# One stream of gate units beside three seven-product pairs, and state updates in pairs of rows, in a two-layer trunk on one Trainium2 core

## The chip, the cores and the metric

The kernel runs on one core of a Trainium2 chip. The metric is the device time of one execution in microseconds (us); lower is better. Engines are named as in the profile: PE is TensorE (PEld its weight loads), DVE is VectorE, ACT is ScalarE, POOL is GpSimd, and SP is SyncE, which here only issues DMAs.

## The reference

Two layers work on x of 256 tokens by 2048, in float32. Layer 0 (even) has a gated linear recurrence and a dilated attention and is not touched. Layer 1 (odd) is this:

```python
def odd_layer(x, norm, w_in, w_alpha, b_alpha, head_norm, v_norm, w_s, b_s, w_out):
    h = rms_norm(x, norm)
    z = h @ w_in
    q, k, v, a_lr, gc, u, vd, gd = jnp.split(z, split_points(ODD_SIZES), axis=-1)
    log_a = jax.nn.log_sigmoid((a_lr @ w_alpha + b_alpha).astype(F32)) / GLA_TAU
    o = gla_chunked(heads(q, GLA_DK), heads(k, GLA_DK), heads(v, GLA_DV), heads(log_a, GLA_DK))
    yc = rms_norm(o, head_norm).reshape(bsz, seq, GLA_VW).astype(x.dtype) * jax.nn.silu(gc)
    yd = spatial_gating(jax.nn.gelu(u), jax.nn.gelu(vd), w_s, b_s, v_norm) * jax.nn.silu(gd)
    return jnp.concatenate([yc.astype(x.dtype), yd.astype(x.dtype)], axis=-1) @ w_out
```

`gla_chunked` has four heads and four chunks of 64 tokens. Its state goes from chunk to chunk as decay * state + upd, with upd = (k * exp(b_last - b))^T v of one chunk; the output of a chunk is its masked product with v plus q times the state before it. The kernel ends with x + layer 1, normalized.

## The kernel before

Each product with a float32 weight is made of three matmuls on halves: activations and weights are split into a rounded high part and the rest, and high*high, high*low and low*high are added in PSUM. A weight tile comes as one DMA of 128 x 1024 (512 KB) into a slot of `rawp` (10 slots). `parts` (L122) makes its halves: ACT casts it to `whi` (L125, 4 slots) and DVE subtracts to `wlo` (L73, 4 slots). The raw slot is free when the subtraction has ended.

A *unit* is 512 columns of `w_in`. `token_steps` (L146) computes one: 8 steps, each with one weight tile, its two halves of 512 columns and, for both token blocks, three matmuls each (L133 to L135), 12 matmuls of 512 columns. `by_token` runs such steps alone.

`pair` (L199) computes two units together by seven products instead of eight (a Strassen scheme over two token blocks, two units and two halves of the rows). Its 28 steps each have one weight tile and 6 matmuls (L227 to L229): steps 1 to 4 on tiles x0, 5 to 8 on y0, 9 to 12 on x0, 13 to 16 on y0, 17 to 20 on x0, 21 to 24 on z0, 25 to 28 on x0. The sums of weights are made by the DMAs: after the halves of a tile are made, POOL issues a DMA that adds another weight tile to it in place (L221, 16 per pair), and the tile is used again 8 steps later. x0 and y0 are loaded ahead (L214), z0 behind step 16, so a pair holds eight raw slots of the ten. The sums of activations are made once for all three pairs by `make_forms` (L679) on DVE and ACT, in 8 pieces; the first pair needs the first of them at its fifth step.

Side work is written as generators. `spawn` starts one; a yield of n gives way until n ticks have passed; `tick` is called with the matmuls, two ticks per pair step and four per token step of 512 columns. `drain` runs all that is left. The order in which an engine gets its instructions is then made by the framework's scheduler, which puts them roughly in program order and moves one ahead when it reckons that its inputs are ready.

Layer 1 runs in this order: `w_va` (a quarter of v and the decay's input, 272 columns), unit 0 (another quarter of v, 256 columns), with `make_forms` and `decay` (L630) as side work; then `weave` (L169) of the pair of q and k with units 2 (half of v) and 22 (half of the gate gc), 16 token steps spread over the 28 pair steps; `gla` (L759) as side work of the second pair (vd), which has no unit beside it; then the third pair (u) with units 26 (rest of gc) and 38 (half of gd), 16 token steps; then unit 42 (rest of gd) alone; then `w_out1`. At the third pair's start `gla_gate(0)` and `normed` begin as side work; `gla_gate(1)` begins when unit 26 is done. Constants `vn` and `hn` (512 KB each in SBUF) are loaded by POOL between the second and the third pair, `wst` between the first and the second.

PSUM has eight banks in three pools: `psm` (4, the products of by_token and pair), `psa` (2, transposes and small products), `pso` (2, products of units beside a pair, state updates `up` of L787, outputs `op`, and `s_ps`).

Of the kernel before, what the change touches and what calls it, by code (L numbers as in the profile page):

```python
# [16 lines left out]
P = 128  # L17
# [34 lines left out]
def trunk(ctx, tc, x, xt, lead, w_in0, w_out0, w_va, w_in1, w_out1, w_gate, small, dist, cst, w_alpha, w_s,  # L52
# [28 lines left out]
    def big_tile(shape, name):  # L81
        return big.tile(shape, F32, name=name, tag="big")
# [83 lines left out]
            yield  # L166
        return ps

    def weave(pair_steps, units):  # L169

        total, done, taken = 28, 0, 0
        units = list(units)
        count = 8 * len(units)
        result = None
        while True:
            try:
                next(pair_steps)
            except StopIteration as end:
                result = end.value
                break  # L180
            taken += 1
            while units and done * total < taken * count:
                steps, use = units[0]
                try:
                    next(steps)
                    done += 1
                except StopIteration as end:
                    use(end.value)
                    units.pop(0)
        for steps, use in units:  # L190
            while True:
                try:
                    next(steps)
                except StopIteration as end:
                    use(end.value)
                    break
        return result

    def pair(w, ua, ub, act, forms):  # L199

# [476 lines left out]
    forms2 = [(sums2, k0, b) for k0, b in ((0, 0), (8, 0), (8, 1), (0, 1))]  # L677

    def make_forms():  # L679
        for i in range(2):  # L680
            def part(k0, b, lo=0):
                return act2[:, k0 + 4 * i:k0 + 4 * i + 4, lo + b * P:lo + (b + 1) * P].bitcast(F32)

            def plus(o, a, b, op=ALU.add):
                nc.vector.tensor_tensor(out=o, in0=a, in1=b, op=op)  # L685

            def minus(o, a, b):
                plus(o, a, b, ALU.subtract)

            def keep(f, src):  # L690
                _, k0, b = forms2[f]
                split(sums2, slice(k0 + 4 * i, k0 + 4 * i + 4), b * P, P, src)

            s, r = (sp_tile([P, 4, P], n) for n in ("fs", "fr"))
            minus(s, part(0, 1), part(8, 1))
            minus(r, part(0, 1, T), part(8, 1, T))
            plus(s, s, r)
            keep(1, s)
            yield 3
            minus(r, part(0, 0), s)  # L700
            plus(r, r, part(0, 0, T))
            keep(2, r)
            yield 3
            minus(s, part(8, 0), r)
            plus(s, s, part(8, 0, T))
            keep(0, s)
            yield 3
            s, r = (sp_tile([P, 4, P], n) for n in ("fs", "fr"))
            minus(s, part(0, 1), part(0, 0))
            minus(r, part(0, 1, T), part(0, 0, T))  # L710
            plus(s, s, r)
            keep(3, s)
            yield 3
# [9 lines left out]
    ps = by_token(w_in1, 0, act2, n=256)  # L723
    for b in range(2):
        nc.scalar.activation(v1[0][:, b, 256:512], ps[b], AF.Copy, scale=rs1[:, b:b + 1])
    gates = [None, None]

    def spare():
        return [pso.tile([P, 512], F32, name="ps2", tag="o") for _ in range(2)]

    def unit_between(unit, use):
        return token_steps(w_in1, unit, act2, ps=spare()), use

    def keep_v1(ps):
        for b in range(2):
            nc.scalar.activation(v1[1][:, b, :], ps[b], AF.Copy, scale=rs1[:, b:b + 1])

    def keep_gate(c):
        def use(ps):
# [2 lines left out]
                nc.scalar.activation(gates[c][:, b, :], ps[b], AF.Silu, scale=rs1[:, b:b + 1])  # L742
        return use

    ps, ps_k = weave(pair(w_in1, 6, 10, act2, forms2), [unit_between(2, keep_v1), unit_between(22, keep_gate(0))])
    drain()
    eb, enb, ebl = decays
    for b in range(2):
# [2 lines left out]
    for b in range(2):  # L751
        for t in (enb, ebl):
            nc.vector.scalar_tensor_tensor(out=t[:, b, :], in0=ps_k[b], scalar=rs1[:, b:b + 1], in1=t[:, b, :],
                                           op0=ALU.mult, op1=ALU.mult)
    qt, kt, kd = eb, enb, ebl
    osb = []
    gla_ro = []

    def gla():  # L759
# [21 lines left out]
        st = [big_tile([P, 4, T], f"st{c}") for c in range(3)]  # L781
        for h in range(4):
            vs = slice((h % 2) * T, (h % 2) * T + T)
            for c in range(3):
                lo = (c % 2) * 64
                up = pso.tile([P, T], F32, name="up", tag="o")
                nc.tensor.matmul(up, kd[lo:lo + 64, c // 2, h * P:(h + 1) * P], v1[h // 2][lo:lo + 64, c // 2, vs],  # L787
                                 start=True, stop=True)
                if c == 0:
                    nc.scalar.copy(st[0][:, h, :], up)  # L790
                else:
                    nc.vector.scalar_tensor_tensor(out=st[c][:, h, :], in0=st[c - 1][:, h, :],
                                                   scalar=dec[:, h, c:c + 1], in1=up, op0=ALU.mult, op1=ALU.add)
                yield 1
        osb.extend(big_tile([P, 2, 512], f"osb{b}") for b in range(2))
        sso = tiny.tile([P, 2, 4], F32, name="sso", tag="sso", bufs=1)
        for b in range(2):
            for hp in range(2):
                op = pso.tile([P, 2, T], F32, name="op", tag="o")
                for i in range(2):  # L800
                    h = 2 * hp + i
                    vs = slice(i * T, (i + 1) * T)
                    if b:
                        nc.tensor.matmul(op[:, i, :], att[:, b, h, :], v1[hp][:, b, vs], start=True, stop=False)
                    for half in range(2):
                        c = 2 * b + half
                        own = slice(half * 64, half * 64 + 64)
                        if not b:
                            nc.tensor.matmul(op[own, i, :], att[:, b, h, own], v1[hp][:, b, vs],
                                             start=True, stop=(c == 0))  # L810
                        if c:
                            nc.tensor.matmul(op[own, i, :], qtt[:, h, b * P + half * 64:b * P + half * 64 + 64],
                                             st[c - 1][:, h, :], start=False, stop=True)
                nc.scalar.copy(osb[b][:, hp, :], op)
                for i in range(2):
                    square_sum(osb[b][:, hp, i * T:(i + 1) * T], sso[:, b, 2 * hp + i:2 * hp + i + 1])
                yield 2
# [8 lines left out]
                            base=0, channel_multiplier=-1)  # L826
    vf = []
    mv = tiny.tile([P, 8, 2], F32, name="mv", tag="mv", bufs=1)
    for c, ps in enumerate(weave(pair(w_in1, 14, 18, act2, forms2), [])):
        t = big_tile([P, 2, 512], f"vf{c}")  # L830
        for b in range(2):
            nc.scalar.activation(t[:, b, :], ps[b], AF.Gelu_apprx_tanh, scale=rs1[:, b:b + 1])
            for i in range(2):
                bs = tiny.tile([P, 6], F32, name="bs", tag="bs", bufs=2)
                nc.vector.bn_stats(bs, t[:, b, i * T:(i + 1) * T])
                nc.vector.bn_aggr(mv[:, c * 4 + b * 2 + i, :], bs)
        vf.append(t)
# [41 lines left out]
    yd = []  # L879
    spawn(gla_gate(0))  # L880
    spawn(normed(0))
    spawn(normed(1))

    def mix(c, t):
        yield 2
        for b in range(2):
            s_ps = pso.tile([P, 2, T], F32, name="s_ps", tag="o")
            for i in range(2):
                g = 2 * c + i
                nc.tensor.matmul(s_ps[:, i, :], wst[:, g, :], vf[c][:, b, i * T:(i + 1) * T], start=True, stop=True)  # L890
                nc.vector.scalar_tensor_tensor(out=t[:, b, i * T:(i + 1) * T], in0=s_ps[:, i, :],
                                               scalar=sm[:, S_BS + g:S_BS + g + 1], in1=t[:, b, i * T:(i + 1) * T],
                                               op0=ALU.add, op1=ALU.mult)
            yield 2

    def keep_gate1(ps):
        keep_gate(1)(ps)
        spawn(gla_gate(1))

    sgds = [big_tile([P, 2, 512], "sgd0")]  # L900

    def keep_gd0(ps):
        for b in range(2):
            nc.scalar.activation(sgds[0][:, b, :], ps[b], AF.Silu, scale=rs1[:, b:b + 1])

    between = [unit_between(26, keep_gate1), unit_between(38, keep_gd0)]
    for c, ps in enumerate(weave(pair(w_in1, 30, 34, act2, forms2), between)):
        t = big_tile([P, 2, 512], f"yd{c}")
        for b in range(2):
            nc.scalar.activation(t[:, b, :], ps[b], AF.Gelu_apprx_tanh, scale=rs1[:, b:b + 1])  # L910
        yd.append(t)
        spawn(mix(c, t))
# [11 lines left out]


    spawn(sgu_gate(0, 16))
    ps = by_token(w_in1, 42, act2)
    sgds.append(big_tile([P, 2, 512], "sgd1"))
    for b in range(2):
        nc.scalar.activation(sgds[1][:, b, :], ps[b], AF.Silu, scale=rs1[:, b:b + 1])  # L930
    spawn(sgu_gate(1, 1))


# [148 lines left out]
```

## Time and profile before

| | us |
|---|---|
| median of 3 runs | 894.34 (893.6 to 894.72) |
| the profiled execution | 894.46 |
| its span, first to last instruction | 892.7 |
| PE busy | 866.1 (97%) |
| DVE busy | 596.0 (67%) |
| ACT busy | 528.4 (59%) |
| POOL busy | 55.3 (6%) |

The busy time is that of one profiled execution. PE's matmuls are pipelined and their ends are modelled, so a busy PE is not PE at its peak. A wait is put down to whatever ended it. Layer 1 begins near 485 us; its pairs run from about 522, 609 and 671 us on, and the last weights' product ends near 885 us.

### The profile page before, as it was taken

The page shows a single profiled execution, that of the slowest core. Times are in us where ns is not written, and L with a number is a line of the kernel's source. Part 1 is how long each engine was busy: PE and PEld are TensorE (multiplying, and loading weights), DVE is VectorE, ACT ScalarE, POOL GpSimd, SP SyncE. Part 2 cuts the span into 40 slices and gives each one's busy share as a digit, 9 for nine tenths or more (in the row PEclk, how much of TensorE's full clock was granted, in tenths as well). Part 3 has the DMA queues.
Part 4 walks back from the last instruction along what each step waited for, and adds up shares of the span by engine and source line. Part 5 has one row for each costly group of instructions (what it writes and reads, how often), then busy time and mean ns, then how long its engine had stood idle before and what let it go on. Part 6 is the DMA issues. An engine that isn't in the chain of part 4 may idle for free.

```text
span 892.7 us, 11928 instructions
## 1 busy us (share of the span) xinstructions
PE 866.1 (97%) x4408; PEld 725.8 (81%) x4408; DVE 596.0 (67%) x851; ACT 528.4 (59%) x765; POOL 55.3 (6%) x75
## 2 busy tenths in 40 slices
PE   9999999999999999999999799999995999999996
PEld 7888888888888888888888688887574877888886
DVE  7676556586586587666555976687477668665652
ACT  7755556766766756554444586656573556754542
POOL 0100000000000000000000012103111211000000
PEclk9999999999999999999999899999997999999999
DMA  9886655455465365565545479999996999665502
GB/s 345 340 330 207 196 185 165 154 183 174 139 201 166 118 208 175 192 195 188 189 123 168 140 178 251 298 299 216 233 248 175 227 307 307 224 221 193 193 26 94
DMA packets 52138, 182.35 MB, mean 204 GB/s; under 512 B 5856, under 2 KB 6368, under 8 KB 51824
## 3 DMA queue, kind: packets, MB, share of 16 engines
q1 hardware_dynamic: 43776, 152.13, 49.4%
q0 software_dynamic: 8160, 29.40, 16.7%
q8 instruction: 34, 0.56, 0.2%
q14 instruction: 24, 0.20, 0.1%
q10 hardware_dynamic: 144, 0.07, 0.0%
HBM read 179.47 MB, written 2.10 MB: 203 GB/s over the span
## 4 chain that ended last, share of the span: by engine, by line
PE 85%; DMA 6%; DVE 5%; ACT 2%; issue 1%; ACTq 0%; DVEq 0%
PE pc L272 20%; PE ps L134 13%; PE ps L135 12%; PE ps L133 12%; PE pc L271 10%; DMA raw<-in_w_in 6%; PE ps L227 3%; PE ps L229 3%; PE ps L228 3%; DVE wlo L73 2%; ACT whi L125 1%; PE up L787 1%; PE pc L274 1%; DVE fs L685 1%; PE sc L457 1%
## 5 line engine op out<-in xcount | busy, mean ns | idle before, releaser
L73 DVE TENSOR_TENSOR wlo<-raw,whi 128x1024 fp32r<-128x1024 f32 (+1 forms) x320 | 384.0, 1211 | 206.1 <-ACT whi L125 194.5
L125 ACT CAST whi<-raw 128x1024 fp32r<-128x1024 f32 (+1 forms) x320 | 330.3, 1041 | 262.2 <-PE ps L135 102.7
L272 PE MATMUL pc<-act,whi 128*128 128x512 f32 x768 | 269.7, 395 | 0.0
L271 PE MATMUL pc<-act,wlo 128*128 128x256 f32 x720 | 208.7, 290 | 0.0
L272 PEld LDWEIGHTS pc<-act,whi 128*128 128x128 f32 x768 | 142.8, 188 | 29.2
L134 PE MATMUL ps<-wlo,act 128*128 128x512 f32 (+2 forms) x352 | 134.3, 382 | 9.0 <-DVE wlo L73 9.0
L133 PE MATMUL ps<-whi,act 128*128 128x512 f32 (+2 forms) x352 | 133.0, 382 | 7.2 <-ACT whi L125 6.8
L271 PEld LDWEIGHTS pc<-act,wlo 128*128 128x128 f32 x720 | 136.0, 189 | 2.5 <-DVE wlo L73 0.9
L135 PE MATMUL ps<-whi,act 128*128 128x512 f32 (+2 forms) x352 | 133.2, 379 | 0.0
L133 PE MATMUL ps<-whi,yt 128*128 128x512 f32 (+1 forms) x256 | 97.1, 379 | 0.0
L135 PE MATMUL ps<-whi,yt 128*128 128x512 f32 (+1 forms) x256 | 96.4, 377 | 0.0
L134 PE MATMUL ps<-wlo,yt 128*128 128x512 f32 (+1 forms) x256 | 96.3, 376 | 0.0
L134 PEld LDWEIGHTS ps<-wlo,act 128*128 128x128 f32 x352 | 68.4, 194 | 22.1 <-DVE wlo L73 10.7
L133 PEld LDWEIGHTS ps<-whi,act 128*128 128x128 f32 x352 | 67.5, 193 | 20.5 <-ACT whi L125 7.8
L135 PEld LDWEIGHTS ps<-whi,act 128*128 128x128 f32 x352 | 68.4, 194 | 11.4
L221 POOL DMA_DIRECT2D raw<-in_w_in x48 | 41.2, 858 | 308.4 <-DMA raw<-in_w_in 148.1
L135 PEld LDWEIGHTS ps<-whi,yt 128*128 128x128 f32 x256 | 48.2, 188 | 8.9
L134 PEld LDWEIGHTS ps<-wlo,yt 128*128 128x128 f32 x256 | 48.2, 188 | 8.5
L133 PEld LDWEIGHTS ps<-whi,yt 128*128 128x128 f32 x256 | 48.2, 188 | 8.4
L227 PE MATMUL ps<-whi,sums 128*128 128x512 f32 x96 | 39.4, 410 | 0.0
L228 PE MATMUL ps<-wlo,sums 128*128 128x512 f32 x96 | 37.6, 392 | 0.0
L229 PE MATMUL ps<-whi,sums 128*128 128x512 f32 x96 | 37.6, 391 | 0.0
(271 smaller groups left out, 894.1 us busy)
## 6 DMA issues: line engine op xcount, KB each, us to landing
raw<-in_w_in SPq DMA_DIRECT2D x204, 512.0 KB, 5.0
raw<-in_w_out SPq DMA_DIRECT2D x64, 512.0 KB, 4.6
raw<-in_w_in POOLq DMA_DIRECT2D x48, 512.0 KB, 8.7
raw<-in_w_va SPq DMA_DIRECT2D x8, 272.0 KB, 2.6
xs<-in_x SPq DMA_DIRECT2D x2, 1024.0 KB, 5.8
out<-xs SPq DMA_DIRECT2D x8, 256.0 KB, 2.6
first<-in_lead SPq DMA_DIRECT2D x4, 384.0 KB, 4.9
xt<-in_xt SPq DMA_DIRECT2D x6, 256.0 KB, 7.8
```

The lines of the kernel that those rows point to most:

```text
L73: nc.vector.tensor_tensor(out=o, in0=a, in1=hi.bitcast(F32), op=ALU.subtract)
L125: nc.scalar.copy(hi, raw)
L133: nc.tensor.matmul(ps[b], xh, wh, start=first, stop=False)
L134: nc.tensor.matmul(ps[b], xh, wl, start=False, stop=False)
L135: nc.tensor.matmul(ps[b], xl, wh, start=False, stop=last)
L221: nc.gpsimd.dma_start(out=raw, in_=part(u, i), accum_op=ALU.add)
L227: nc.tensor.matmul(ps, xh, wh, start=(first and j == 0), stop=False, skip_group_check=not first)
L228: nc.tensor.matmul(ps, xh, wl, start=False, stop=False, skip_group_check=not first)
L229: nc.tensor.matmul(ps, xl, wh, start=False, stop=(j == 7), skip_group_check=not first)
L271: nc.tensor.matmul(ps[c][:, 1, :], wl, act[:, k, 0:T], start=False, stop=False)
L272: nc.tensor.matmul(ps[c], wh, act[:, k, :], start=(k == 0), stop=(k == KT - 1))
L274: nc.tensor.matmul(ps[c][:, 1, :], wl, act[:, k, 0:T], start=False, stop=False)
```

## The change

Unit 2 (half of v) moves ahead of the first pair and runs alone, so v is whole before the pairs. A class `Stream` holds one row of four units (22, 26, 38, 42: both halves of gc, both of gd) and gives out their steps one by one; `weave` takes 12 of them beside the first pair, 4 beside the second and 12 beside the third, and `stream.finish()` runs the last 4 behind it. `make_forms` begins 6 ticks later. `gla_gate(1)` starts with `gla_gate(0)`. The state updates of chunks 0 and 1 are issued next to each other, on the two halves of the rows; that of chunk 2 takes all 128 rows, for which the second half of `kd`'s second block (chunk 3) is set to zero by POOL. `up`, `op` and `s_ps` move from `pso` to `psa`; `pso` is left to the units.

```diff
+    class Stream:
+        def step(self):
+            if not self.units:
+                return
+            steps, use = self.units[0]
+            if callable(steps):
+                steps = steps()
+                self.units[0] = steps, use
+                self.left = 8
+            next(steps)
+            self.left -= 1
+            if not self.left:
+                self.units.pop(0)
...
+    def weave(steps, stream, count):
+        done = taken = 0
+        while True:
+            try:
+                next(steps)
+            except StopIteration as end:
+                return end.value
+            taken += 1
+            while done * 28 < taken * count:
+                stream.step()
+                done += 1
...
     def make_forms():
+        yield 6
...
+    ps = by_token(w_in1, 2, act2)
+    for b in range(2):
+        nc.scalar.activation(v1[1][:, b, :], ps[b], AF.Copy, scale=rs1[:, b:b + 1])
...
+    stream = Stream([between(22, keep_gate(0)), between(26, keep_gate(1)), between(38, keep_gd(0)),
+                     between(42, keep_gd(1))])
+    ps, ps_k = weave(pair(w_in1, 6, 10, act2, forms2), stream, 12)
     drain()
...
+    nc.gpsimd.memset(kd[64:P, 1, :], 0.0)
...
-            for c in range(3):
-                lo = (c % 2) * 64
-                up = pso.tile([P, T], F32, name="up", tag="o")
...
+            ups = [psa.tile([P, T], F32, name="up", tag="a") for _ in range(2)]
+            for c in range(2):
+                own = slice(c * 64, c * 64 + 64)
+                nc.tensor.matmul(ups[c], kd[own, 0, h * P:(h + 1) * P], v1[h // 2][own, 0, vs], start=True, stop=True)
+            nc.scalar.copy(st[0][:, h, :], ups[0])
+            nc.vector.scalar_tensor_tensor(out=st[1][:, h, :], in0=st[0][:, h, :], scalar=dec[:, h, 1:2], in1=ups[1],
+                                           op0=ALU.mult, op1=ALU.add)
+            yield 2
+            up = psa.tile([P, T], F32, name="up", tag="a")
+            nc.tensor.matmul(up, kd[:, 1, h * P:(h + 1) * P], v1[h // 2][:, 1, vs], start=True, stop=True)
+            nc.vector.scalar_tensor_tensor(out=st[2][:, h, :], in0=st[1][:, h, :], scalar=dec[:, h, 2:3], in1=up,
+                                           op0=ALU.mult, op1=ALU.add)
+            yield 2
...
-                op = pso.tile([P, 2, T], F32, name="op", tag="o")
+                op = psa.tile([P, 2, T], F32, name="op", tag="a")
...
-    for c, ps in enumerate(weave(pair(w_in1, 14, 18, act2, forms2), [])):
+    for c, ps in enumerate(weave(pair(w_in1, 14, 18, act2, forms2), stream, 4)):
...
     spawn(normed(0))
+    spawn(gla_gate(1))
     spawn(normed(1))
...
-            s_ps = pso.tile([P, 2, T], F32, name="s_ps", tag="o")
+            s_ps = psa.tile([P, 2, T], F32, name="s_ps", tag="a")
...
-    for c, ps in enumerate(weave(pair(w_in1, 30, 34, act2, forms2), between)):
+    for c, ps in enumerate(weave(pair(w_in1, 30, 34, act2, forms2), stream, 12)):
...
     spawn(sgu_gate(0, 16))
-    ps = by_token(w_in1, 42, act2)
+    stream.finish()
     spawn(sgu_gate(1, 1))
```

## Rows read from the trace of the kernel before

**Rows 1.** Busy time by stage: stretch, length, engines (x instructions), granted clock, DMA, GB/s.

```profile
484.00:522.00 38.00, 32.10 (x214) 29.22 (x213) 34.95 (x55) 24.12 (x36) 0.90 (x1) 0.91 0.47 147
609.00:671.00 62.00, 61.10 (x271) 40.57 (x268) 41.67 (x51) 40.13 (x60) 13.96 (x17) 1.00 0.99 234
671.00:692.00 21.00, 12.13 (x38) 9.17 (x39) 16.72 (x38) 7.58 (x8) 1.94 (x3) 0.76 0.60 158
```

**Rows 2.** PE's waits, 484 to 522: who, for whom, total us, times, longest.

```profile
PE ps L134 <- DVE wlo L73: 4.8, 3, 3.1
PE ps L133 <- ACT whi L125: 1.0, 1, 1.0
```

**Rows 3.** PE's waits from 609 to 745.

```profile
PE ps L133 <- ACT whi L125: 5.8, 2, 5.5
PE ps L134 <- DVE wlo L73: 4.0, 2, 3.2
PE ps L228 <- DVE wlo L73: 0.8, 2, 0.5
```

**Rows 4.** Busy time and granted clock of three stretches at half clock.

```profile
498.40:504.20 5.80, 5.72 (x25) 5.72 (x26) 5.60 (x10) 1.89 (x4) 0.00 (x0) 0.51 0.59 191
676.40:681.60 5.20, 5.17 (x14) 3.97 (x15) 3.04 (x4) 4.05 (x4) 0.87 (x1) 0.50 0.45 115
688.50:691.80 3.30, 3.27 (x8) 2.59 (x9) 3.30 (x4) 0.00 (x0) 0.88 (x2) 0.50 0.52 161
```

**Rows 5.** Chain of waits, 664 to 706: start, us, engine or DMA, tile.

```profile
665.62 9.61 DMA raw<-in_w_in
...
692.51 8.35 DMA raw<-in_w_in
...
703.30 8.57 DMA raw<-in_w_in
```

**Rows 6.** Timeline of PE, first pair: start, us; a token step, then two pair steps.

```profile
541.73 0.40 PE L133 MATMUL ps<-whi,act 128*128 128x512 f32 x1
...
544.47 0.39 PE L227 MATMUL ps<-whi,sums 128*128 128x512 f32 x1
...
547.19 0.39 PE L133 MATMUL ps<-whi,act 128*128 128x512 f32 x1
```

**Rows 7.** Timeline of PE: two state updates in a row, of 12.

```profile
617.57 0.70 PE L787 MATMUL up<-vv,ebl 64*128 64x256 f32 x2
...
619.09 0.70 PE L787 MATMUL up<-vv,ebl 64*128 64x256 f32 x2
```

**Rows 8.** Chain of waits: a float32 matmul of 128 rows in layer 0.

```profile
151.27 0.43 PE gp L540 x2
```

**Rows 9.** Timeline of PE, 636 to 637: matmuls of 64 columns.

```profile
636.51 0.38 PE L809 MATMUL op<-vv,att 128*64 128x256 f32 x1
636.52 0.38 PE L812 MATMUL op<-st,qtt 128*64 128x256 f32 x1
```

**Rows 10.** Tile `up`, who reads it: ns min/median/max, first and last start.

```profile
L792 DVE SCALAR_TENSOR_TENSOR st<-st,dec,up x8: 475/478/481, 619.9 to 635.1; 128x256 f32<-128x256 f32 x8
```

**Rows 11.** Groups of instructions, 484 to 522: count, busy us, mean ns, idle before.

```profile
L73 DVE TENSOR_TENSOR wlo<-raw,whi 128x1024 fp32r<-128x1024 f32 x6 | 7.2, 1220 | 0.9 <-ACT whi L125 0.9
```

**Rows 12.** Timeline of SP's issues: start, us from first to last, line, count.

```profile
656.41 8.40 SPq L214 DMA_DIRECT2D raw<-in_w_in  x6
665.62 1.46 SPq L119 DMA_DIRECT2D raw<-in_w_in  x2
```

**Rows 13.** DMA queues and issues, 522 to 609: share of 16 engines; median us to landing.

```profile
q0 software_dynamic: 2388, 8.67, 52.3%
q1 hardware_dynamic: 4016, 14.63, 44.9%
...
raw<-in_w_in SPq DMA_DIRECT2D x28, 512.0 KB, 7.4
raw<-in_w_in POOLq DMA_DIRECT2D x17, 512.0 KB, 9.4
```

## What the change was predicted to do

> **What bounds the kernel now.** I read the page first: TensorE (PE) is busy 97% of the span, so only two things can shorten the kernel, less PE work or fewer moments in which PE waits. The slices show where it waits: a dip at about half the span and one at three quarters. The table by stage confirms it [rows 1]: from 609 to 671 us PE is busy 61.10 of 62.00 us, but from 671 to 692 only 12.13 of 21.00, at a granted clock of 0.76; from 484 to 522 it is 32.10 of 38.00 with the clock at 0.91. The waits say what ended those gaps. In the first stage PE waits 4.8 us for weight splits on VectorE (DVE) and 1.0 us for a cast [rows 2], while DVE is busy 34.95 of 38 us: there DVE is the limit, because the sums for the pairs (`make_forms`) and layer 1's decay run on it beside the splits. Around the end of the middle pair PE waits 5.8 us for a cast (5.5 in one piece) and 4.0 us for a split (3.2 in one piece) [rows 3]. After each long wait the clock stands at half, its lower level of 1.2 GHz, for 5.8, 5.2 and 3.3 us [rows 4]; shorter waits, near 1 us, brought no such stretch. At half clock half of the stretch is lost: 2.8 + 2.6 + 1.65 us.
>
> So the forms stage loses 5.8 + 2.8 = 8.6 us. The change from middle to third pair loses 5.5 + 3.2 + 0.8 [rows 3] + 4.25 = 13.8 us. The second waits of rows 3's first two lines, 0.3 + 0.8 = 1.1 us, lie in the third pair.
>
> The chain of waits names the cause of the 5.5 us: a DMA of weights, issued at 665.62, that took 9.61 us [rows 5]. It is the raw tile of the first unit step beside the third pair.
>
> **What the change leaves alone.** Both kernels have the pairs by seven products, and the same units; only the order changes. A token step is 12 matmuls in 2.74 us, two pair steps the same [rows 6]. Beside the three pairs' 28 steps each stood 16, 0 and 16 token steps and 8 behind; now 8 stand in front, then 12, 4, 12 and 4. PE's sum is the same, save for the state updates.
>
> **State updates.** Before: 12 matmuls `up`, each with three other matmuls between. From one to the next are 1.52 us [rows 7]; less three at 0.228 (2.74 / 12) an `up` costs 0.84 us, 10.0 us in all. Now each head has two 64-row matmuls one behind the other and one of 128 rows. The second costs between 0.43 us (a 128x256 one of 128 rows in layer 0 [rows 8]) and 0.84. The two of 64 rows cost between 0.84 (side by side) and 1.68 (in turn); the nearest rows are those of `op`, where matmuls on two halves of the array start 0.01 us apart [rows 9], though those are halves of columns, not of rows. A head thus costs 1.27 to 2.52 us against 2.51: 0 to 5.0 us saved; I take 0.65 x 4 = 2.6. The Trainium skill ("TensorEngine Tiling (Array Packing)", Tiling Modes, Key Properties) says that row tiles work independently and that a change of mode drains the array; by that a head costs about 1.3 us and the saving is 4.8 us. Only the columns' case is in this trace. Against it: `psa` has two banks, and a head's first two updates take both. The third needs the bank that ScalarE (ACT) copies; the next head's need both DVE updates (0.48 us each [rows 10]), which queue behind a split of 1.22 us [rows 11]: 2.2 us, where four pair products (2 ticks) give 1.36 us. That is 0 to 0.8 us of waiting per head, 0 to 3.2; I take 0.7, for the pair's other products can be queued in between. The same page (Restrictions and Gotchas, PSUM Pressure) warns of this: row tiles write different banks.
>
> The memset of half of `kd` goes to POOL, busy 13.96 of 62 us here [rows 1]. Queued behind it are the load of `wst` and the middle pair's first accumulating DMAs. `kd` needs only two of the pair's sums that are done 8 steps before its end, so it runs there. If it were late, the accumulations would start late; their tiles are next read 8 steps on. 0, with 0 to 2 us for the range.
>
> **Forms stage.** `make_forms` starts 6 ticks later and v (unit 2) follows, whose 8 steps give DVE 2.74 us each for one split. The DVE work up to the last split of unit 0 stays nearly the same, for 21 ticks of forms still fall in it. What it need no longer do by then: two splits of the pair's weights and one of the decay's operations on 1024 elements, 3 x 1.22 = 3.7 us of 34.95. Against it, work lands later and bunches up in unit 0. I take 3.0 us saved; at best all 8.6 go (subtractions overtake the forms), at worst one more split comes late, 1.2 us lost.
>
> **Middle to third pair.** Ten raw slots; a pair holds eight. The last unit raw can be loaded only when the slots of the next pair's eight are given out. Before: six loads in 8.40 us from 656.41, then the unit's [rows 12]; it lands at 675.23, 18.8 us after the first. Prices from the first pair's DMA queues: q0 52.3% of 87 us for 17 accumulations, 2.68 us each; q1 44.9% for 28 loads, 1.40 each [rows 13]. In the 18.8 us fall seven loads (9.8), two accumulations (5.4) and the two constant rows `vn` and `hn` (2.0 each, between the two prices): 19.2, which fits. After the change four unit raws run in the middle pair and take a slot; only one of the next pair's tiles, not two, is loaded ahead: one load more, 20.2 us. PE has, from the same moment, 9 pair steps (12.3) + one unit step (2.74) + a lead of 0.7 to 1.9 = 15.7 to 16.9 us, where it had 14.5. With a cast (half of the 2.4 us that lie between landing and next load, 10.79 - 8.35, in rows 5) the wait is 20.2 + 1.2 - 16.3 = 5.1 us: the long wait stays, with its half clock. The 0.8 us for splits go, as each unit step gives DVE 1.5 us. `gla_gate(1)` now also starts here: about 3.1 us more of DVE (by element counts from rows 10 and 11), partly under the DMA wait; I take 0.2 us of it. Sum 0.4 + 0.8 - 0.2 = 1.0 us saved; ends 13.8 saved and 3.1 lost.
>
> **Third pair.** The 1.1 us there hung on the late unit raws and on `gla_gate(1)`, which moves away: 1.1 saved (0 to 1.1).
>
> **Denser pairs.** For 12 of the steps each pair step brings an accumulation. With 12 units PE needs 1.37 + 0.43 x 2.74 = 2.54 us, DMA 2.68 + 0.43 x 1.40 = 3.28: a backlog of 8.9 us after 12 steps. Before it was 12 x (3.48 - 2.93) = 6.6 us, and the first pair bore it with no wait. A tile is next read 20.3 us later, so it should hold. Unit raws run in a loop of 10.8 us for two [rows 5]; two units now take 11.8 us of PE, before 10.2. 0 to 4 us lost, I take 1.0 for the second pair's first unit raw.
>
> At the end only four unit steps (16 ticks) remain ahead of the output, as many as `gla_out` needs: 0, or 2 us if a transpose is late, as `s_ps` now shares `psa` with them.
>
> **Sum.** Against the profiled run's 894.46 us (span 892.7 + 1.8 around it; the median is 894.34): - 2.6 + 0.7 - 3.0 - 1.0 - 1.1 + 1.0 = 888.5 us.
>
> **Rivals.** *No gain.* The updates' saving is eaten by the wait for their banks, and `gla_gate(1)` costs its 3.1 us at the third pair's start: - 3.0 + 3.1 - 1.1 + 1.0 = 0, 894.5 us. For it: DVE is where the second wait came from. Against: it idles while the raw is awaited. *Slower.* The loads of unit raws share the DMA engines with denser accumulations. A landing may take 11.83 - 2.4 = 9.4 us; it took 8.35 to 8.57 [rows 5], accumulations 9.4 in the median [rows 13]. Each us above costs 12 us (12 loops of two in pairs 1 and 3); my other gains are 7.0, so it decides from 10.0 us on; at 10.5 the time is 894.46 - 7.0 + 13 = 900.5. Against this stands a rule of the Trainium skill ("DMA: Bandwidth & Descriptors", Queues, rings and completion order): each engine takes packets from its queues in turn, so SP's loads would not stand behind POOL's backlog. By it the 13 us are nothing. *The whole gap goes.* If the first unit raw gets a slot ahead of the third pair's second four tiles, or the constants land earlier, all 13.8 go, 12.8 more than forecast: 875.7 us. *Not what it says:* the words promise seven products for the pairs; they are in both, and nothing is counted for that.
>
> **Chances.** Forecast 0.56, no gain 0.15, slower 0.14, gap gone 0.15. Of the forecast's own spread (882 to 894) a tenth is within 0.2%, about what a measurement tells from no change. Faster 0.72, same 0.12, slower 0.16. From 875 to 900 no more than 2 in 10 is left out.
>
> **What would show it.** Right: `up` rows two at a time, a head under 2 us; v's unit with no PE wait; a wait of 4 to 6 us for a cast at the third pair's first unit, half clock behind it. Wrong: PE waits for a unit's cast in mid-pair, or landings over 9.4 us (slower rival); no half clock near the third pair (gap gone); PE waiting for `st` (banks).

## The result, and the profile after

| | median of the runs | profiled execution, span |
|---|---|---|
| before | 893.97 us (893.46 to 894.72) | 894.46, 892.7 |
| after | 916.98 us (913.44 to 919.49) | 913.44, 911.7 |

The ratio is 1.0254, with a 95% interval from 1.021 to 1.0297: the change costs 2.5%, where 0.65% was to be gained. The profiled execution of after is the fastest of its four; the two traces differ by 19.0 us. The four executions of after lie at 913.4, 914.7, 919.3 and 919.5 us, so differences of a few us are read from the stages of the profiled executions as well.

The first step is to find the stage. The table takes four moments from each trace (the first matmul of pair 2 and of pair 3, the last matmul of pair 3, the last of all) and takes off 2.74 us for each unit step that has run by then [rows 6], since the kernels put their unit steps in different places. What is left is compared with before, stage by stage. An example: pair 2 starts at 626.46 in after with 20 unit steps done and at 607.03 in before with 16, so (626.46 - 54.80) - (607.03 - 43.84) = +8.5.

| us against before | up to pair 2 | pair 2 | pair 3 | behind | sum |
|---|---|---|---|---|---|
| after | +8.5 | -3.1 | +13.7 | -0.1 | +19.0 |

So the middle pair, with the paired updates, is shorter, and pairs 1 and 3, the ones beside which 12 unit steps stand in place of 16, are longer. PE's waits from 560 to 790 us in after (who, for whom, total us, times, longest):

```profile
PE ps L133 <- ACT whi L125: 19.0, 3, 8.9
PE s_ps L916 <- DVE vf L901: 5.1, 2, 4.5
PE ps L238 <- DVE wlo L73: 3.9, 2, 3.1
```

Three waits for a cast make up 19.0 us. One, of 3.7, is the known one at the start of the third pair (5.5 in before [rows 3]). The others, of 6.4 and 8.9, are new and lie in the middle of pairs 1 and 3. The stages show them (columns as in rows 1): full speed just ahead of the first, then the first, the third pair's start, and the last.

```profile
570.00:588.00 18.00, 18.00 (x82) 14.88 (x81) 10.36 (x9) 8.53 (x9) 3.24 (x4) 1.00 1.05 278
588.00:606.00 18.00, 11.10 (x39) 8.38 (x38) 8.13 (x7) 9.49 (x10) 4.08 (x5) 0.81 0.76 195
690.00:722.00 32.00, 18.48 (x58) 12.89 (x57) 24.53 (x53) 13.27 (x15) 2.61 (x3) 0.80 0.54 180
750.00:772.00 22.00, 12.68 (x48) 9.72 (x47) 7.73 (x7) 7.66 (x8) 3.25 (x4) 0.77 0.80 223
```

The chain of waits of after names what ended the two (start, us, what):

```profile
581.46 12.38 DMA raw<-in_w_in
...
750.68 14.53 DMA raw<-in_w_in
```

Both are raw tiles of a unit step. Where they stand on SP's queue is seen in its timeline (start, us from the first issue to the last, line, count), first of after, then of before, around the same step:

```profile
563.78 4.42 SPq L119 DMA_DIRECT2D raw<-in_w_in  x2
573.95 5.60 SPq L224 DMA_DIRECT2D raw<-in_w_in  x4
581.46 18.54 SPq L119 DMA_DIRECT2D raw<-in_w_in  x4
```

```profile
548.37 9.85 SPq L119 DMA_DIRECT2D raw<-in_w_in  x3
559.25 6.09 SPq L214 DMA_DIRECT2D raw<-in_w_in  x4
567.98 12.00 SPq L119 DMA_DIRECT2D raw<-in_w_in  x4
```

L224 (L214 in before) are the four `z0` loads, L119 the unit raws. The order is the same in both; what differs is how long the first two raws behind `z0` take from issue to landing (DMA issues of that moment: tile, queue, count, KB, median us to landing), in before and in after. The first line of each shows what else the DMA engines carried just then: q0 is POOL's queue with the accumulations (packets, MB, share of the 16 engines).

```profile
q0 software_dynamic: 1, 0.00, 0.0%
...
raw<-in_w_in SPq DMA_DIRECT2D x2, 512.0 KB, 5.5
```

```profile
q0 software_dynamic: 80, 0.27, 66.8%
...
raw<-in_w_in SPq DMA_DIRECT2D x2, 512.0 KB, 12.3
```

The theory that the experiments test (theory Q in the expectations): with 12 unit steps a pair's accumulations are issued in less PE time, and the DMA engines are still busy with them when `z0` and the unit raws behind it are issued. PE reaches that unit step before its tile is there, and stands.

### The profile page after: what moved, and what is told of

It reads as the page before. It is cut to its first block, busy times and chain, and to the rows that moved or that the text cites. A ratio compares the mean times of both kernels' runs of the same rounds, so it can differ in the third digit from the quotient of the medians.

```text
span 911.7 us, 11935 instructions
## 1 busy us (share of the span) xinstructions
PE 865.7 (95%) x4408; PEld 726.9 (80%) x4408; DVE 596.5 (65%) x851; ACT 527.2 (58%) x764; POOL 56.1 (6%) x76
## 4 chain that ended last, share of the span: by engine, by line
PE 84%; DMA 6%; DVE 6%; ACT 2%; issue 1%; ACTq 0%; DVEq 0%
PE pc L282 19%; PE ps L134 13%; PE ps L135 12%; PE ps L133 12%; PE pc L281 9%; DMA raw<-in_w_in 6%; PE ps L237 3%; PE ps L238 3%; PE ps L239 3%; DVE wlo L73 2%; ACT whi L125 1%; PE pc L284 1%; PE sc L467 1%; PE gp L551 1%; PE gp L550 1%
## 5 line engine op out<-in xcount | busy, mean ns | idle before, releaser
L133 PEld LDWEIGHTS ps<-whi,act 128*128 128x128 f32 x352 | 67.5, 194 | 33.2 <-ACT whi L125 20.2
L135 PEld LDWEIGHTS ps<-whi,act 128*128 128x128 f32 x352 | 67.9, 193 | 11.4
```

What stands on the lines that cost most here:

```text
L133: nc.tensor.matmul(ps[b], xh, wh, start=first, stop=False)
L135: nc.tensor.matmul(ps[b], xl, wh, start=False, stop=last)
```

## The experiments

### The paired updates alone

In the kernel before: `up` two at a time, `up` and `op` from `psa`, half of `kd` set to zero.

```diff
-                up = pso.tile([P, T], F32, name="up", tag="o")
+            ups = [psa.tile([P, T], F32, name="up", tag="a") for _ in range(2)]
...
-                op = pso.tile([P, 2, T], F32, name="op", tag="o")
+                op = psa.tile([P, 2, T], F32, name="op", tag="a")
```

> The kernel before the change, with the state updates in pairs of rows alone (and up and op in psa, and the half of kd set to zero). Theory: a head's updates take 1.3 to 1.4 us of PE instead of 2.5 with no wait for a bank, so the run is 4 to 5 us shorter than before, near 890. Rival (banks): two banks are too few, PE waits up to 0.8 us per head, and the gain is 1 to 2 us. Rival (the gap takes it): the middle pair ends sooner while the raw tile of the third pair's first unit lands when it did, the wait of 5.5 us grows by what was saved, and the run stays within 1 us of before.

Measured: 887.09 us against 893.76, ratio 0.9927 (0.991 to 0.9944): 6.7 us saved. By stage -0.4, -3.4, -1.7, 0.0. The cost of a head is read in PE's timeline of after, between pair products that else start 0.23 us apart (start, us, line):

```profile
643.53 0.40 PE L239 MATMUL ps<-whi,sums 128*128 128x512 f32 x1
643.86 0.70 PE L810 MATMUL up<-vv,ebl 64*128 64x256 f32 x4
644.49 0.50 PE L237 MATMUL ps<-whi,sums 128*128 128x512 f32 x1
644.83 0.39 PE L238 MATMUL ps<-wlo,sums 128*128 128x512 f32 x1
```

From 643.53 to 644.83 are 1.30 us; less two steps of 0.228 the two `up` of 64 rows cost 0.84, as much as one did in before. The one of 128 rows costs 0.43. Worked out so for all eight groups, the updates cost 5.5 us in after (9.98 in before), 5.9 here, with no PE wait for a bank. So 4.1 of the 5.6 us by stage are PE's; 1.7 lie in pair 3, at whose start the cast is awaited 4.5 us and not 5.5: the gap didn't take the gain. (The profiled execution, 888.9 us, is the slowest of its four; what the others saved beyond it isn't shown.)

### Fewer accumulations

In the kernel after, the four accumulating DMAs of steps 9 to 12 are left out.

```diff
-        yield from run(m56, f5, x0, True, ub + 2)
+        yield from run(m56, f5, x0, True)
```

> The kernel after the change without the four accumulating DMAs of steps 9 to 12 of each pair (that part of the pairs' sums is left out), everything else the same. Theory Q: these 4 x 2.68 = 10.7 us of DMA per pair are the backlog in which z0's loads and the unit raws behind them get stuck; without them the waits of 6.4 and 8.9 us in mid-pair go, with their half clock, and the run takes 893 to 899 us. Rival (order alone): SP's four z0 loads ahead of the unit raws are enough; the waits shrink by less than half and the run stays above 907.

Measured: 897.85 us, 19.1 less than after; by stage +1.3, -1.5, +2.8, -0.1. Both waits in mid-pair are gone; of the waits for a cast, one of 4.0 at the third pair's start and one of 0.8 are left. The two raws behind `z0` land like this:

```profile
raw<-in_w_in SPq DMA_DIRECT2D x2, 512.0 KB, 5.0
```

In that moment q0 carried no packet. SP's order is unchanged, `z0` still stands in front; so the order alone is not the cause, the accumulations in flight are.

### 16, 0 and 12 unit steps

```diff
-    ps, ps_k = weave(pair(w_in1, 6, 10, act2, forms2), stream, 12)
+    ps, ps_k = weave(pair(w_in1, 6, 10, act2, forms2), stream, 16)
...
-    for c, ps in enumerate(weave(pair(w_in1, 14, 18, act2, forms2), stream, 4)):
+    for c, ps in enumerate(weave(pair(w_in1, 14, 18, act2, forms2), stream, 0)):
```

> The kernel after the change, with 16 unit steps beside pair 1, none beside pair 2, 12 beside pair 3 and 4 behind (instead of 12, 4, 12 and 4), and one more buffer for the big tiles, which the earlier end of the second unit needs. Theory Q: with 16 unit steps PE is busy long enough for the accumulations to drain, so the wait of 6.4 us in pair 1 falls below 1.5 us, the one of 8.9 us in pair 3 stays, and the run takes 903 to 908 us. Rival: the wait hangs on what v in front or the stream itself changed, not on how dense the unit steps are; then both waits stay and the run is at 914 to 919.

Measured: 902.83 us, 14.2 less than after; by stage +1.8, -3.6, +10.0, -0.1. Waits from 560 to 790:

```profile
PE ps L133 <- ACT whi L125: 11.9, 2, 9.3
PE ps L238 <- DVE wlo L73: 5.0, 2, 4.1
```

Pair 1's wait is gone, pair 3's (9.3) stays, as expected. Between the two profiled executions 6.6 us went up to pair 2; another 3.7 went in pair 3, at whose start the wait for `vf` fell from 5.1 to 0.2 us.

### 12, 4, 16 and 8: the mirror of it

`v` goes back into the stream as its first unit (and `gla_gate(1)` starts when its gate is there, in pair 3).

```diff
-    stream = Stream([between(22, keep_gate(0)), between(26, keep_gate(1)), between(38, keep_gd(0)),
+    stream = Stream([between(2, keep_v1), between(22, keep_gate(0)), between(26, keep_gate1), between(38, keep_gd(0)),
...
-    for c, ps in enumerate(weave(pair(w_in1, 30, 34, act2, forms2), stream, 12)):
+    for c, ps in enumerate(weave(pair(w_in1, 30, 34, act2, forms2), stream, 16)):
```

> The kernel after the change with v back as the first unit of the stream: 12 unit steps beside pair 1, 4 beside pair 2, 16 beside pair 3 and 8 behind. Theory Q: pair 1 is as thin as in the changed kernel and keeps its wait of 6 to 7 us; pair 3 is as dense as before the change and loses its wait of 8.9 us and its half clock; the run takes 903 to 909 us. Rival: the wait in pair 3 comes from how that pair starts (the late raw tiles, VectorE's queue) and stays, and the run is at 912 to 918.

Measured: 903.19 us, 13.8 less than after; by stage +8.9, -2.4, +2.2, +0.8. Now pair 1 keeps its wait (7.5 us) and pair 3's is gone. The wait follows the count of unit steps beside a pair, not which units they are. That few unit steps alone do not make it is seen in pair 2 of after, which has 4 and no such wait: its one unit raw behind `z0` was issued at 665.80 and landed at 670.44, and PE took that step up at 684.03 only.

### 14, 2 and 14

The same two lines and the third pair's, with 14, 2 and 14.

> The kernel after the change with 14 unit steps beside pairs 1 and 3 and 2 beside pair 2 and behind (instead of 12, 4, 12, 4). Theory Q as a sum: two more unit steps bring PE 5.5 us of work and DMA 2.8 us of loads, of which about half fall ahead of the stall, so each wait in mid-pair shrinks by 2 to 4 us, to some 3 to 6 us, and keeps part of its half clock; the run takes 903 to 910 us. Rival (a step): once a unit lies behind z0's loads it waits the same however many came before, both waits stay at 6 to 9 us and the run is at 913 to 918; or they vanish at once and it is below 900.

Measured: 915.48 us, no better than after; the waits in mid-pair are 6.4 and 9.9. The rival held by the time, but the trace shows a second cause under it:

```profile
PE ps L133 <- ACT sgd L760: 9.9, 1, 9.9
PE ps L133 <- ACT sgc L753: 6.4, 1, 6.4
```

ACT's timeline there:

```profile
594.67 1.04 ACT L125 CAST whi<-raw 128x1024 fp32r<-128x1024 f32 x1 [9.02 <-DMA raw<-in_w_in]
595.74 1.28 ACT L753 ACT_TABLE_LOAD   x1
597.03 1.27 ACT L753 ACTIVATE sgc<-ps,rs 128x512 f32<-128x512 f32 x2
```

With 14 the step that finds no data is the first of a new unit. It needs banks that ACT still has to read for the unit before, and that read (Silu, with a table load) stands on ACT's queue behind the late cast. The cast could have let PE go at 595.7; PE went at 597.8, when the first Silu was done. So the data was late by about 2 us less than in after, and ACT's order took them again.

### z0 one tile per step

```diff
-        load(z0, ua + 2)
-        yield from run(m56, f6, x0, False, ua + 2)
+        yield from run(m56, f6, x0, False, ua + 2, (z0, ua + 2))
```

> The kernel after the change, with one thing moved: the four z0 tiles of a pair are no longer loaded in one block behind step 16, but one in each of the steps 17 to 20. Theory Q (the queue): the waits of 6.4 and 8.9 us in mid-pair (pairs 1 and 3) come from the two unit raws that stand on SP's queue behind z0's four loads while the accumulations are still in flight; then each wait falls to 0 to 2 us, its stretch at half clock goes with it, and the run takes 895 to 905 us against 917. Rival D (too little DMA time): data is short all the same, PE then waits as long in front of z0's own products some steps later, and the run stays at 911 to 919.

Measured: 907.0 us, 10.0 less than after, between the two expectations; by stage +5.1, -2.6, +12.0, -0.1. The waits in mid-pair are 3.0 and 5.2 us and are again put down to ACT's reading of the last unit's banks. The order on SP's queue is worth about half of the two waits (15.3 us in after, 8.2 here); that the backlog makes the other half is argued from the run with fewer accumulations.

### Where s_ps lies

```diff
-            s_ps = psa.tile([P, 2, T], F32, name="s_ps", tag="a")
+            s_ps = psm.tile([P, 2, T], F32, name="s_ps", tag="ps")
```

> The kernel after the change, with s_ps alone taken from the pool psm instead of psa. Theory H (hoisted): s_ps stands early on PE's queue because psa has a bank free then, and PE waits 5.1 us for VectorE's normed rows in front of it, with a stretch at half clock behind; in psm it comes later, that wait goes and the run takes 908 to 912 us. Rival (VectorE is late in any case): PE then waits as long for the next weight split, and the run stays at 914 to 919.

Measured: 917.6 us, the same. My theory H fell. PE's waits from 690 to 730:

```profile
PE ps L238 <- DVE wlo L73: 5.1, 2, 4.3
PE tp L874 <- DVE osb L884: 4.0, 2, 2.4
PE ps L133 <- ACT whi L125: 3.4, 1, 3.4
```

The wait for `vf` is gone, and other waits for DVE have come in its place.

### VectorE's order at the third pair's start

First `gla_gate(1)` alone is put off by 24 ticks; then `rv` and `normed(0)` by 8 and `normed(1)` by 32 as well, in smaller portions.

```diff
-    spawn(gla_gate(1))
+    spawn(gla_gate(1, 24))
...
     def normed(c):
+        yield 8 + 24 * c
+        if not c:
+            rv.append(rsqrt_of(mv[:, :, 1], 8, 1.0, "rv"))
+            yield 2
```

> The kernel after the change with the second head gate (gla_gate(1)) put off by 24 ticks from the third pair's start, and nothing else. Theory G: its six operations, about 3 us of VectorE, stand ahead of the weight splits and of the normalising of vf in VectorE's queue; without them PE waits some 3 us less at that place (5.1 us for vf and 3.9 us for splits now), and the run takes 912 to 914 us. Rival: the order behind the reciprocal of rv decides, the same waits stay, and the run is at 916 to 918.

> The run with gla_gate(1) put off, and rv and normed put off by 8 ticks and in smaller portions as well. Theory V: the waits for vf and for splits at the third pair's start (9.0 us together) and a part of the stretches at half clock behind go; the two waits in mid-pair stay; the run takes 905 to 910 us. Rival: the third pair's mid-pair wait takes up what is saved, as the raw tile there lands when it did, and the run is at 913 to 918.

Measured: 911.29 us (5.7 less than after), and 907.16 us (9.8 less). In the stage of pair 3 the profiled executions give less for the first: +11.4 and +5.3 against before, where after has +13.7, so 2.3 and 8.4. PE's waits from 690 to 730, first of the one, then of the other:

```profile
PE ps L133 <- ACT whi L125: 3.7, 1, 3.7
PE ps L238 <- DVE wlo L73: 2.6, 2, 1.9
PE ps L237 <- ACT whi L125: 2.6, 2, 1.8
PE s_ps L918 <- DVE vf L903: 1.4, 2, 0.8
```

```profile
PE ps L133 <- ACT whi L125: 4.0, 1, 4.0
PE ps L237 <- ACT whi L125: 0.8, 1, 0.8
PE ps L238 <- DVE wlo L73: 0.8, 1, 0.8
```

What had happened is in DVE's timeline of after (start, us, line, tile, idle before): `gla_gate(1)` (the `sgc` and `osb` rows come from both gates), a wait for ACT's square root, and `normed`, all ahead of the next weight split at 716.49.

```profile
706.54 1.29 DVE L880 TENSOR_TENSOR sgc<-sgc,hn 128x512 f32<-128x512 f32 x2
707.75 0.88 DVE L884 SCALAR_TENSOR_TENSOR osb<-osb,ro,sgc 128x256 f32<-128x256 f32 x2
709.84 0.20 DVE L298 RECIPROCAL rv<-rv 128x8 f32<-128x8 f32 x1 [1.22 <-ACT rv L297]
...
710.31 1.05 DVE L899 TENSOR_SCALAR vf<-vf,mv,rv 128x256 f32<-128x256 f32 x3
...
716.49 1.22 DVE L73 TENSOR_TENSOR wlo<-raw,whi 128x1024 fp32r<-128x1024 f32 x1
```

The split before that one ran at 702.30. Theories G (some 3 us) and V hold: the same work, put off, takes most of these waits away.

### Towards a faster kernel

From the kernel with the paired updates alone: the third pair's `y0` tiles one per step; then DVE's work put off there and in `make_forms`; then the statistics and the first gate put off too.

```diff
-    for c, ps in enumerate(weave(pair(w_in1, 30, 34, act2, forms2), between)):
+    for c, ps in enumerate(weave(pair(w_in1, 30, 34, act2, forms2, True), between)):
...
-        yield from run(m12, (act, 0, 0), x0, True, ub)
+        yield from run(m12, (act, 0, 0), x0, True, ub, (y0, ub + 2) if spread else None)
```

In the second, `normed` as above, and `yield 3` in `make_forms` becomes `yield 6`.

> The kernel before the change with the paired state updates (the run at 887.1 us), and in the third pair alone the four y0 tiles loaded one in each of its first four steps instead of all before it. Theory S (slots): the first unit's raw tile lands late because it gets a slot behind all eight of the pair's tiles; it now stands ahead of three of them, so the wait of 4.5 us for its cast, the 0.9 us ahead of it and the stretch of 6.8 us at half clock behind it go, and the run takes 876 to 880 us. Rival V (VectorE): the splits at that place queue behind the reciprocal of rv and the normalising of vf, so the wait of 3.2 us for a split grows by what is saved, and the run stays at 884 to 887.

> The run with y0 spread in the third pair, and two things put off on VectorE: rv and normed start 8 ticks later and come in smaller portions, and make_forms has 6 ticks between its parts instead of 3, so that its last ones run beside the first pair. Theory: the waits for splits at these two places come from the order of VectorE's work, not from its sum; the 3.2 us at the third pair's start and some 5 us of waits in the forms stage go with their stretches at half clock (3.4 us lost in the latter), and the run is 6 to 11 us below the one with y0 spread alone. Rival: VectorE has too much work in both stages in any case; the waits move some steps on and the run is within 2 us of it.

> The run with VectorE's work put off (879.1 us), and two more pieces put off at the third pair's start: the statistics of vf and the first head gate (gla_gate(0)) come in portions some ticks later instead of all at once. Theory V: the waits that are left there (0.9, 0.7 and 2.2 us for splits and the stretch of 3.4 us at half clock behind) come from these operations standing ahead of the splits on VectorE's queue; they go, and the run takes 874 to 877 us. Rival: the raw tiles are the next thing to be late, PE waits for casts in their place, and the run stays within 1.5 us of 879.

Measured: 884.7, 879.13 and 878.7 us (before 893.77, 893.77 and 893.69); the last two are 0.9829 (0.9812 to 0.9846) and 0.9811 (0.9768 to 0.9854) of before. By stage (up to pair 2, pair 2, pair 3) -0.3, -3.6, -5.9, then -4.4, -2.2, -7.7, then -2.7, -3.6, -8.9. With `y0` spread the wait of 4.5 us for the cast is gone, but PE waits for splits in its place (rival V, 2.4 us gained instead of 7 to 11): from 640 to 790 us

```profile
PE ps L228 <- DVE wlo L73: 4.4, 4, 2.1
PE ps L134 <- DVE wlo L73: 1.1, 2, 0.8
```

The second is 5.6 us below the first, just short of its 6 to 11. With `make_forms` spaced by 6 ticks, the forms stage (484 to 545) has hardly a wait left, where before had 5.8 us up to 522 [rows 2], and 4.1 us are gained up to pair 2:

```profile
PE ps L134 <- DVE wlo L73: 0.6, 1, 0.6
PE ps L228 <- DVE wlo L73: 0.2, 1, 0.2
```

The waits for splits around the third pair's start stayed in that run (4.1 us for the pair's). Putting off the statistics as well left 1.7 of them, and casts were then late instead (4.3 us from 560 to 790, 3.3 of them in the third pair): the rival of the last expectation, no gain.

## Why the prediction was wrong, point by point

**Denser pairs: this step failed.** It computed a backlog of 8.9 us after 12 steps (6.6 before) and held it against the next reader of an accumulated tile, 20.3 us later. That reader did hold: no wait of PE stands ahead of one. But the backlog lies on the same DMA engines as SP's loads. For the unit raws the step asked only whether a loop of two has room on average, with the landings of before (8.35 us) as they were. The nearest reader is the unit step behind `z0`, whose raws took 12.38 and 14.53 us: the wrong deadline was checked. Its 1.0 us (0 to 4) came out at some 18: without four of the accumulations 7.2 us are gone up to pair 2 (+8.5 to +1.3) and 10.9 in pair 3 (+13.7 to +2.8).

**The slower rival** had the cause right (landings over 9.4 us, from 10.0 on it decides) and the price wrong. It counted 12 loops that are each a little late, 900.5 us. In fact 2 loops are late by much, the two behind `z0` (12.38 and 14.53 us), and each wait brought a stretch at half clock (granted 0.50 from 595 to 600 us). Its room of 9.4 us for a landing was too wide as well. The raw was issued at 581.46; PE stood for it from 588.60 on (595.04 less the wait of 6.44):

```profile
595.04 0.80 PE L133 MATMUL ps<-whi,act 128*128 128x512 f32 x1 [6.44 <-ACT whi L125]
```

From landing (593.84) to PE's start 1.2 us go for the cast, so the tile had 5.9 us. A landing of 5.0 us, as in the run with fewer accumulations, fits into that; 12.38 doesn't. The rule of the Trainium skill weighed there ("DMA: Bandwidth & Descriptors", Queues, rings and completion order: an engine takes packets from its queues in turn) would have made the loads' delay nothing. No run here shows the turns themselves, but the same two raws on the same queue landed in 5.0 us with four accumulations fewer and in 12.3 with them: in turn or not, sharing the engines costs, and that decides.

**State updates: right in kind, two terms mis-sized.** 4.5 us of PE were saved, not 2.6, as three heads cost 1.27 us each, the lower end, and the first 1.69; the bank wait of 0.7 was 0. (Its 1.36 us are six pair products, not the four that the text names.) Alone on the kernel before the part is worth 6.7 us. The Trainium skill ("TensorEngine Tiling (Array Packing)", Tiling Modes, Key Properties) had given 4.8 by its rule that row tiles work independently, and the trace agrees: 0.84 us for two of 64 rows, as for one. A third of the saving has another source, though: the update that takes all 128 rows, half of them zero, costs 0.43 us, and one of 64 rows alone 0.84. Why the smaller one costs more isn't shown.

**Forms stage: the term failed.** 3.0 us were to be saved. In the two runs with `v` in front and no stall in pair 1, the time up to pair 2 is 1.3 and 1.8 us more than before. In after itself waits of 5.8 us and half of 3.4 us (518.0 to 521.4, granted clock 0.51) make 7.5, where before lost 8.6: about 1 us saved. The difference between these goes with the clock there (last section). The splits were indeed less late (1.5 us, 4.8 in before [rows 2]), but the decay, whose sums ran beside the first pair before and now run ahead of it, became what PE waits for. Waits of after from 484 to 545:

```profile
PE bp L665 <- ACT lah L660: 3.3, 1, 3.3
PE ps L134 <- DVE wlo L73: 1.5, 2, 0.9
PE at_ps L644 <- DVE alr L731: 1.0, 1, 1.0
```

**Middle to third pair.** The wait for the cast was forecast at 5.1 us and is 3.7, by the mechanism named: from the first of seven loads (679.77) to the unit's landing (701.12) are 21.4 us (20.2 forecast), and PE stood after 18.9 of them (16.3). The 0.8 us for splits, which were to go, became 3.9. `gla_gate(1)` was put at 0.2 us because DVE idles while the raw is awaited; it cost 2.3 us by stage (5.7 by the medians), for it runs after that wait, ahead of the splits. The "no gain" rival named this and priced it at 3.1, about right. `rv` and `normed` behind it cost another 6.1 by stage, which no term had.

**Third pair, end.** In after the 1.1 us can't be told apart from the stall that came there; in the run with fewer accumulations no wait over 0.3 us is left behind the third pair's start, so they seem to be gone as forecast. Behind the pairs nothing changed (-0.1), as forecast.

The range, 875 to 900, left the result out: its upper end came from a rival whose price was too low.

## What to carry to other kernels

When compute between transfers is taken away, find for each queue the transfer with the least slack behind the new backlog, not only the readers of the backlog itself. Late data stops engines that work in order: what stands behind the late cast, a bank's release included, is late with it. Deferred work of a vector engine is cheap only where it does not stand ahead of the splits that the next matmuls need.

## What the runs showed of the hardware

The same waits brought different clocks. After and the run with `s_ps` in `psm` have the same matmuls in the same order up to here, and the same three waits between 497 and 502 us (0.7, 1.0 and 0.9 us). Yet from 502.8 to 512.8 us the granted clock was at its upper level in the one and at half in the other (columns as in rows 1):

```profile
502.80:512.80 10.00, 10.00 (x70) 8.43 (x69) 9.75 (x14) 5.99 (x7) 0.00 (x0) 1.00 0.45 147
```

```profile
502.80:512.80 10.00, 10.00 (x35) 7.23 (x34) 7.42 (x11) 3.30 (x4) 0.00 (x0) 0.50 0.29 102
```

The wait for `lah` that follows is 3.3 us in the one and 1.8 in the other, where PE comes to it later. So the prediction's reading that waits near 1 us bring no such stretch held in the trace it was read from, not in these runs. Up to pair 2 four runs with the same code there came out at +7.9 and +8.5 us with the clock at 1.00 from 502.8 to 512.8, and at +10.7 and +11.6 with 0.50. What sets the clock apart was not found; differences of some 3 us between two profiled executions of this stage say nothing of an edit.
